# The last two sums of the seventh product's weights, at the front of VectorE's queue instead of its end

## The chip, the cores and the metric

The kernel runs on one core of one Trainium2 chip. The metric is the device time of one execution in microseconds (us). Lower is better.

## The reference

Every token is multiplied with the weights of all eight experts, and the results are added up with the softmax of the router's logits as factors:

```python
probs = softmax(router_logits)                    # 16 x 512 tokens, 8 experts
for e in range(8):
    output += probs[:, :, e:e+1] * np.matmul(x, expert_weights[e])   # 512 -> 2048 columns
```

Inputs and output are float32. Seen as one product, it is an 8192 x 4096 matrix (each token's 512 values times each of its eight factors) by a 4096 x 2048 matrix (the experts' weights below each other).

## The kernel before, in words

**Two levels of a seven-product scheme.** The big product is computed by a scheme of Strassen's kind: 2 x 2 blocks are multiplied with seven products instead of eight, and sums and differences of blocks are formed before and after. The outer level splits the tokens into blocks `a` and `b` of 256, the experts into two halves and the columns into two halves of 1024. Its products are called P1 to P7 here (`product(r, q)`, r = 1 to 7; q = 0 to 15 numbers the pairs of token blocks). The inner level does the same once more inside each product, with the seven steps `STEPS = (1, 5, 6, 2, 7, 3, 4)`. Each step is eight matmuls of 128 x 128 by 128 x 512 in float16 into one bank of PSUM. Some stages have a third level (`Thirds`); those near the change have none.

**Stages and slots.** `stages` is a list of pairs of products. `run(stage)` goes through the seven steps and takes one step of each product in turn, so a stage has 14 slots, the even ones of its first product and the odd ones of its second. Three stages matter here:

- stage k7: P6 for q = 15 (even slots) and P7 for q = 0 (odd slots), the first P7;
- stage k7+1: P4 for q = 0 (even) and P7 for q = 1 (odd);
- stage k7+2: P4 for q = 1 and P7 for q = 2.

In stage k7 slots 8 and 9 are step 7 of P6 and of P7, slots 12 and 13 are step 4.

**The right-hand side of a step** is a tile of 128 x 4096 float16, a block of weights or a difference of blocks (`inner_sums`). For P7 four blocks called t3 are fetched, and VectorE makes four differences of them: the sums for steps 5, 6, 7 and 4. Each is one instruction (`step`, L107). The sum for step 6 reads that for step 5, the sum for step 4 reads that for step 6, and the sum for step 7 is written over a block that the sum for step 5 reads. They are made once and serve all 16 P7.

**The left-hand side** (`Left`) is made anew for each product: two tiles `z` (experts' factors times x; for P7 a tile `u` of the other token block is subtracted from each), then `s2` (tile name `d`), the difference of the halves of the first, and `i` (a tile named `z` again, `z<-z,d` in the profile), the second minus `s2`. Step 6 reads `s2`, steps 7 and 3 read `i`.

**VectorE's queue.** VectorE runs its instructions in the order in which the kernel issues them. That order is written by a planner at build time. `later(cost, make, first=False)` puts a task at the end of `queue`, or with `first=True` at its front. `slack()`, once a slot, takes tasks off the front as long as VectorE's planned clock is behind TensorE's. `need(task)`, called by `Left.op` and `Right.op` right before a step's matmuls, takes everything off the front up to and including the task that the step reads. Additions that end a step (`post`, `h<-ps,h` in the profile) are issued directly, behind the step. `run` queues a stage's `i` tiles when the stage begins, and after the first slot (`queue_lefts`) the left sides of the next stage; both go to the end of the queue.

**Loads.** SyncE's queue issues the loads of x and factors (`xT`, `pT`) for the stage after next at slot 1 (`start_loads`), and the base blocks that a product's results are added to (`Base.fetch`, tile `h`). The last base block of P7 for q = 0, (1, 0), is issued at slot 3 of stage k7, behind those loads. `xT` and `pT` share a pool of 10 buffers, and a load waits until VectorE has read the buffer's old contents. ScalarE's queue issues the loads of P4's weights, 1 MB each (`turnover(k7, 0, 4, "t4")`, `fetch_w`, L164), at slots 1, 4, 7, 10 and 13 of stage k7 and at slot 2 of the next. In the built program the DMAs of these two queues take eight completion counters in turn, and a DMA waits until the one that had its counter before has landed. GpSimd's queue issues the stores of results (`out_dram<-h`).

Nearly all of VectorE's work has line 107 (`tt`), all steps' matmuls have line 130 (`mm`), and the tiles tell them apart. What the diff touches:

Of the kernel before, what the change touches and what calls it, by code (L numbers as in the profile page):

```python
# [31 lines left out]
def kernel(  # L32
# [73 lines left out]
    def tt(o, a, b, op):  # L106
        dve(nc.vector.tensor_tensor(out=o, in0=a, in1=b, op=op))  # L107
# [15 lines left out]
    def bank():  # L123
        return psum.tile([P, NB], f32, name="ps", tag="ps")

    def bank2():
        return psum.tile([P, NB], f32, name="pt", tag="pt", bufs=2)
# [6 lines left out]
    def new_w():  # L134
        return wpool.tile([P, K8, NB], f16, name="w", tag="w")

    def new_u():
        return zpool.tile([P, K8, HQ], f16, name="u", tag="u", bufs=1)

    def new_z():  # L140
        return zpool.tile([P, K8, HQ], f16, name="z", tag="z")
# [25 lines left out]
    def inner_sums(b, t7=None):  # L167

        w = {1: b[0, 0], 2: b[1, 0], 3: b[1, 1], 7: t7 or b[0, 1]}

        def step(p, x, y):
            if p not in w:
                w[p] = new_w()
            tt(w[p], x, y, SUB)
        return w, {5: lambda: step(5, b[0, 1], b[0, 0]), 6: lambda: step(6, b[1, 1], w[5]),
                   4: lambda: step(4, b[1, 0], w[6]), 7: lambda: step(7, b[1, 1], b[0, 1])}
# [145 lines left out]
    for n in range(2):  # L322
        ps = [bank2() if n == 0 and j < 2 else bank() for j in range(4)]
        for e in range(HE):
# [4 lines left out]
            if n == 0 and e == 2:  # L329
# [3 lines left out]
                w, sums = inner_sums(b11, new_w())  # L333
# [36 lines left out]
    def flush(task):  # L370
        while task is not None and not task.done:
            queue.popleft().run()

    def need(task):
        if task is not None and not task.done:
            flush(task)
            clock["pe"] = max(clock["pe"], clock["dve"])

    def later(cost, make, first=False):
        t = Task(cost, make)  # L380
        (queue.appendleft if first else queue.append)(t)
        return t
# [58 lines left out]
    def times(z, k, xb, pb):  # L441
        tt(z.rearrange("p (e c) t -> p e c t", e=2), xb.t.unsqueeze(1).to_broadcast([P, 2, C, HQ]),
           pb.t[:, ds(2 * k, 2)].unsqueeze(2).to_broadcast([P, 2, C, HQ]), MUL)

    class Left:
# [6 lines left out]
        def make(self, k):  # L452
            if self.of is not None:
                need(self.of.task[k])
            t = self.t[k] = new_z()
            times(t, k, self.xb, self.pb)
            if self.less is not None:
                u = new_u()
                times(u, k, *self.less)
                tt(t, t, u, SUB)  # L460
            if self.of is not None:
                tt(t, self.of.t[k], t, SUB)
            if self.kept is not None:
                tt(t, t, self.kept.t[:, ds(k * K8, K8), :], SUB)
# [80 lines left out]
    class Right:  # L545
# [6 lines left out]
            self.w, sums = inner_sums(b)  # L552
            return sums

        def queue_sum(self, sums, p):
            self.task[p] = later(2.29, sums[p])

        def op(self, p):
            need(self.task.get(p))
# [94 lines left out]
    def at(stage, slot, make):  # L654
        hooks.setdefault((stage, slot), []).append(make)

    def add(*products):
        stages.append(products)
        return len(stages) - 1


    right = {r: Right() for r in (2, 5, 6, 7, 4, 3)}
# [33 lines left out]
    def product(r, q, **how):  # L696
        left, loads = left_of(r, q)
        lefts[r, q] = left
        p = None
        if r == 1:  # L700
            def sink(tn, o):
                pool(kept_rows(q)(tn), o)
            p = Product(right[1], left, sink)
        elif r == 2:
            if q >= ON_BASE:
                bases[2, q] = Base(kept_rows(q))
            p = Product(right[2], left, to_out(q, 0, 0), bases.get((2, q)))
        elif r == 5:
            bases[6, q] = m1 = Base(kept_rows(q))
            m1.task = {}  # L710

            p = Product(right[5], left, to_out(q, 1, 0))
        elif r == 6:
            m1 = bases[6, q]

            def base(tn):
                need(m1.task[tn])
                return m1.t[tn]
            p = Product(right[6], left, to_out(q, 0, 1), base)
        elif r == 7:  # L720
            base = bases[7, q] = Base(lambda tn: out_rows(q, 0, 1, tn))
            p = Product(right[7], left, to_out(q, 1, 1), base)
        elif r == 4:
            p = Product(right[4], left, to_out(q, 1, 0, accum_op=ADD), products[7, q].o.__getitem__)
        else:
            p = Product(right[3], left, to_out(q, 0, 1, accum_op=ADD), **how)
        p.loads = loads
        products[r, q] = p
        return p
# [137 lines left out]
    k7 = add(some, product(7, 0))  # L867
# [79 lines left out]
    for kn, where in zip(((0, 0), (0, 1), (1, 1), (1, 0)), ((1, 8), (3, 2), (5, 0), (5, 9))):  # L947
        at(*where, lambda kn=kn: cast21(kn))

    def sums_at(stage, slot, r, of, ps):  # L950
        def go():
            if right[r].w is None:
                right[r].sums = right[r].build(of)
            for p in ps:
                right[r].queue_sum(right[r].sums, p)
        at(stage, slot, go)
    sums_at(ND - 1, 3, 2, b21, (5,))
    sums_at(ND - 1, 5, 2, b21, (6,))
    sums_at(ND - 1, 7, 2, b21, (7,))
    sums_at(ND - 1, 12, 2, b21, (4,))  # L960
    ODD = 0, 1
    for i, (kn, e) in enumerate((kn, e) for kn in (ODD, (0, 0), (1, 1), (1, 0)) for e in range(2)):
        stage = ND + i - 2 if kn != ODD else 2 + 2 * i
        wedge_at(stage, 2, kn, e, (stage + 1, 0))

    def fetch_at_w(stage, slot, of, what, kn):
        at(stage, slot, lambda: of.__setitem__(kn, fetch_w(what, kn)))
# [101 lines left out]
    def turnover(stage, place, r, raw, every=3):  # L1069

        right[r].w = {}

        def fetch(p):
            if p in RAW:
                right[r].w[p] = fetch_w(raw, RAW[p])
            else:
                right[r].w[p] = fetch_w((r, p), (0, 0))
        if every == 3:
            at(stage - 1, 9, lambda: fetch(1))
        for i, p in enumerate(STEPS[every == 3:]):  # L1080
            at(*slots_after(stage, place + 1, every * i), lambda p=p: fetch(p))
    t3 = {}
    for slot, kn in zip((0, 2, 4, 6), ORDER):
        fetch_at_w(k7 - 1, slot, t3, "t3", kn)
    for stage, slot, p in ((k7 - 1, 10, 5), (k7 - 1, 13, 6), (k7, 3, 7), (k7, 7, 4)):
        sums_at(stage, slot, 7, t3, (p,))
    turnover(k7, 0, 4, "t4")
    turnover(k3 - 1, 1, 3, "b22", 2)

# [119 lines left out]
```

## Time and profile before

| | us |
|---|---|
| time, median of 3 runs | 1374.52 (1374.25 to 1374.65) |
| the profiled execution's own time | 1374.57 |
| its span, first to last instruction | 1372.5 |
| TensorE busy (matmuls) | 1355.9 |
| VectorE busy | 1130.7 |
| ScalarE, GpSimd busy | 258.8, 435.8 |

Times in the profile are counted from the first instruction. `z<-xT,pT` means that an instruction writes a tile of that name and reads the two others; buffer numbers are left out. In a timeline the first two columns are start and duration, and an idle time of the engine ahead of the instruction stands in brackets with what ended it. One instruction's duration reaches some 0.08 us into the next one's, so that what an instruction costs in a row of them is the distance of two starts. A matmul's modelled end lies 0.16 us behind the start of the next.

### The profile page before, as it was taken

What the parts mean: (1) busy time and instruction counts of PE and PEld (TensorE: products, weight loads), DVE (VectorE), ACT (ScalarE), POOL (GpSimd) and SP (SyncE); (2) the same over time, 40 slices, a digit from 0 to 9 for tenths busy, and PEclk for the clock granted to TensorE, in tenths of its full rate; (3) what the DMA queues carried; (4) which work ended last, traced back from release to release, by engine and by line L of the source; (5) the groups of instructions that cost most, each with busy time, mean ns of one, the idle gap of its engine ahead of it and who ended that gap; (6) DMA issues with size and microseconds to landing.
All of it is one profiled execution on the core that took longest, in us unless ns stands there. A gap on an engine that the chain in (4) does not pass through costs nothing.

```text
span 1372.5 us, 18682 instructions
## 1 busy us (share of the span) xinstructions
PE 1355.9 (99%) x6822; PEld 665.0 (48%) x6822; DVE 1130.7 (82%) x1365; ACT 258.8 (19%) x517; POOL 435.8 (32%) x667
## 2 busy tenths in 40 slices
PE   9999999999999999999999889999999999999998
PEld 4555545565544444444444334444444444556554
DVE  7876677878899888887878987888989888898884
ACT  3233313242211111111111100000000000233331
POOL 3223323332222323223221113344443434233341
PEclk9999999999999999999999989999999999999999
DMA  9999979898999999999987977999999999999997
GB/s 183 245 218 266 246 222 227 256 243 248 255 333 290 281 311 288 281 262 298 299 265 266 345 257 192 229 255 264 255 265 234 270 259 308 336 304 247 207 159 136
DMA packets 190683, 353.55 MB, mean 258 GB/s; under 512 B 52992, under 2 KB 81920, under 8 KB 185856
## 3 DMA queue, kind: packets, MB, share of 16 engines
q0 software_dynamic: 89824, 189.31, 59.1%
q1 hardware_dynamic: 97456, 139.86, 33.8%
q10 hardware_dynamic: 3312, 23.20, 4.4%
q8 instruction: 53, 0.87, 0.3%
q14 instruction: 38, 0.31, 0.1%
HBM read 208.44 MB, written 180.55 MB: 283 GB/s over the span
## 4 chain that ended last, share of the span: by engine, by line
PE 98%; DVE 1%; DMA 0%; issue 0%; POOL 0%; ACT 0%; DVEq 0%; POOLq 0%
PE ps L130 74%; PE pt L130 24%; DVE z L107 1%; DMA w<-in_x_dram 0%; DVE h L107 0%; DVE u L107 0%; DVE w L107 0%; DVE d L107 0%; DVE z L255 0%; POOL w L121 0%; ACT h L1155 0%; DVE lg L295 0%; DVEq L107 0%; POOLq L1193 0%
## 5 line engine op out<-in xcount | busy, mean ns | idle before, releaser
L130 PE MATMUL ps<-w,z 128*128 128x512 f16 (+1 forms) x3768 | 822.1, 375 | 10.9 <-DVE w L107 10.9
L130 PEld LDWEIGHTS <-z 128*128 128x128 f16 x5272 | 516.0, 98 | 590.5 <-issue 13.7
L121 POOL DMA_DIRECT2D out_dram<-h x380 | 256.0, 706 | 698.8 <-ACT h L614 274.2
L130 PE MATMUL pt<-w,z 128*128 128x512 f16 (+1 forms) x1504 | 317.9, 359 | 0.0
L107 DVE TENSOR_TENSOR z<-xT,pT 128x2048 f16<-128x2048 f16 x220 | 265.9, 1216 | 3.5 <-PE pt L130 2.6
L107 DVE TENSOR_TENSOR h<-ps,h 128x512 f32<-128x512 f32 x248 | 168.9, 687 | 95.4 <-PE ps L130 75.3
L130 PE MATMUL ps<-w,d 128*128 128x512 f16 x880 | 199.1, 379 | 0.0
L601 ACT COPY h<-ps 128x512 f32<-128x512 f32 x118 | 69.2, 586 | 420.2 <-PE ps L130 394.3
L130 PEld LDWEIGHTS <-d 128*128 128x128 f16 x880 | 86.0, 98 | 100.1
L107 DVE TENSOR_TENSOR z<-z,d 128x2048 f16<-128x2048 f16 x110 | 131.8, 1216 | 0.0
L107 DVE TENSOR_TENSOR h<-pt,h 128x512 f32<-128x512 f32 x125 | 85.2, 687 | 50.9 <-PE pt L130 49.2
L107 DVE TENSOR_TENSOR w<-w 128x1024 f16<-128x1024 f16 (+2 forms) x105 | 112.3, 1086 | 1.9 <-PE ps L130 1.0
L614 ACT COPY h<-ps 128x512 f32<-128x512 f32 x50 | 29.3, 586 | 402.5 <-PE ps L130 364.6
L107 DVE TENSOR_TENSOR d<-z 128x1024 f16<-128x1024 f16 x110 | 74.6, 684 | 4.5 <-PE ps L130 3.4
L107 DVE TENSOR_TENSOR ps<-ps,h 128x512 f32<-128x512 f32 (+1 forms) x88 | 51.0, 582 | 26.7 <-PE ps L130 23.3
L597 ACT COPY h<-ps 128x512 f32<-128x512 f32 x95 | 52.6, 605 | 70.7 <-PE ps L130 70.7
L121 POOL DMA_DIRECT2D kept<-h x56 | 30.7, 548 | 93.9 <-ACT h L601 53.8
L121 POOL DMA_DIRECT2D out_dram<-kept x56 | 56.4, 1042 | 12.2 <-DMA out_dram<-h 6.3
L593 ACT COPY ps<-ps 128x512 f32<-128x512 f32 x59 | 33.6, 570 | 121.0 <-PE ps L130 65.3
L107 DVE TENSOR_TENSOR ps<-pt,h 128x256 f32<-128x256 f32 x36 | 15.5, 432 | 38.7 <-PE pt L130 26.6
L107 DVE TENSOR_TENSOR h<-h 128x512 f32<-128x512 f32 (+2 forms) x69 | 45.1, 675 | 1.1 <-DMA h<-kept 0.9
L107 DVE TENSOR_TENSOR z<-z,u 128x2048 f16<-128x2048 f16 x36 | 44.1, 1225 | 1.2
(73 smaller groups left out, 543.9 us busy)
## 6 DMA issues: line engine op xcount, KB each, us to landing
out_dram<-h POOLq DMA_DIRECT2D x380, 256.0 KB, 7.3
pT<-p_dram SPq DMA_DIRECT2D x126, 256.0 KB, 7.2
w<-wd ACTq DMA_DIRECT2D x22, 1024.0 KB, 9.5
xT<-x SPq DMA_DIRECT2D x80, 256.0 KB, 7.5
h<-kept SPq DMA_DIRECT2D x72, 256.0 KB, 8.2
h<-out_dram SPq DMA_DIRECT2D x68, 256.0 KB, 6.0
w<-in_expert_weights_dram POOLq DMA_DIRECT2D x33, 512.0 KB, 10.2
kept<-h POOLq DMA_DIRECT2D x56, 256.0 KB, 5.2
```

What stands on the lines that cost most here:

```text
L107: dve(nc.vector.tensor_tensor(out=o, in0=a, in1=b, op=op))
L121: note(nc.gpsimd.dma_start(out=o, in_=i, **how))
L130: note(nc.tensor.matmul(ps, z, w, start=start, stop=stop, skip_group_check=True))
L593: act(nc.scalar.copy(self.banks["b"], x))
L597: act(nc.scalar.copy(o[tn], q if p == 5 else x))
L601: act(nc.scalar.copy(o[TN[p]], b if p == 2 else x))
L614: act(nc.scalar.copy(o[tn], b))
```

## The change

The sums for P7's steps 7 and 4 are queued one slot later than before (4 and 8 instead of 3 and 7 of stage k7), and at the front of the queue instead of its end. As a task at the front could be run ahead of a sum that it depends on, `queue_sum` now runs that one first if it is still queued. The sums for steps 5 and 6, and those of the other products, are queued as before.

```diff
-        def queue_sum(self, sums, p):
-            self.task[p] = later(2.29, sums[p])
+        def queue_sum(self, sums, p, first=False):
+            def make():
+                flush(self.task.get({6: 5, 7: 5, 4: 6}.get(p)))
+                sums[p]()
+            self.task[p] = later(2.29, make, first)
...
-    def sums_at(stage, slot, r, of, ps):
+    def sums_at(stage, slot, r, of, ps, first=False):
...
-                right[r].queue_sum(right[r].sums, p)
+                right[r].queue_sum(right[r].sums, p, first)
...
-    for stage, slot, p in ((k7 - 1, 10, 5), (k7 - 1, 13, 6), (k7, 3, 7), (k7, 7, 4)):
-        sums_at(stage, slot, 7, t3, (p,))
+    for stage, slot, p in ((k7 - 1, 10, 5), (k7 - 1, 13, 6), (k7, 4, 7), (k7, 8, 4)):
+        sums_at(stage, slot, 7, t3, (p,), p in (7, 4))
```

Built, both programs have the same instructions in the same order on TensorE, ScalarE, GpSimd and SyncE. On VectorE the order differs from stage k7 on for about four stages and is then the same again. This is the order from the end of step 6 of P6 in stage k7, one instruction or group each:

| before | after |
|---|---|
| end of P6 step 6 | end of P6 step 6 |
| a subtraction `h<-h` for P6 | **sum 7** |
| `i` of P6 | end of P7 step 6 |
| end of P7 step 6 | `h<-h` for P6 |
| `i` of P7 | `i` of P6 |
| P4's left: `z`, `d`, `z` | **sum 4** |
| end of P6 step 7 | end of P6 step 7 |
| P7's next left: `z`, `u`, `z<-z,u`, `d` | `i` of P7 |
| and `z`, `u`, `z<-z,u` | P4's left: `z`, `d` |
| **sum 7**, **sum 4** | end of P7 step 7 |
| end of P7 step 7 | P4's left: `z` |
| ends of P6, P7 step 3, P6, P7 step 4 | end of P6 step 3 |
| `i` of P4 | P7's next left: `z`, `u`, `z<-z,u` |
| end of P4 step 1 | ends of P7 step 3, P6 step 4, P7 step 4 |
| `i` of the next P7 | end of P4 step 1 |
| end of the next P7's step 1 | next P7's left: `d`, `z`, `u`, `z<-z,u` |
| and so on | end of the next P7's step 1, and so on |

The completion counters come out otherwise too. Before, the load of the weights for P4's step 7 has the counter of the base block (1, 0) of P7 for q = 0 and waits for its landing. After, the loads for P4's steps 7, 3 and 4 have counters of loads that were issued at the beginning of stage k7. In both programs the loads for steps 3 and 4 also wait for their buffers, until P6's steps 7 and 3 have read what is in them.

## Prediction

> **What bounds the kernel now.** I read the busy times first, then the waits, then TensorE's timeline around the one long wait.
>
> ```profile
> PE 1355.9 (99%) x6822; PEld 665.0 (48%) x6822; DVE 1130.7 (82%) x1365; ACT 258.8 (19%) x517; POOL 435.8 (32%) x667
> PE 98%; DVE 1%; DMA 0%; issue 0%; POOL 0%; ACT 0%; DVEq 0%; POOLq 0%
> PE ps L130 <- DVE w L107: 10.9, 1, 10.9
> ```
>
> TensorE (PE) is busy for 1355.9 of 1372.5 us and makes up 98% of the chain that ended last. Of its 16.6 us of idle time one single wait is 10.9: matmuls that waited for a tile `w` written by VectorE, a sum of weights. Only time in which TensorE stands or runs slowly can be won.
>
> ```profile
> 772.29 3.62 PE L130 MATMUL pt<-w,z 128*128 128x512 f16 x16
> 775.74 3.62 PE L130 MATMUL ps<-w,d 128*128 128x512 f16 x16
> 779.20 5.34 PE L130 MATMUL ps<-w,z 128*128 128x512 f16 x24
> 795.46 3.57 PE L130 MATMUL ps<-w,z 128*128 128x512 f16 x8 [10.92 <-DVE w L107]
> 798.82 3.79 PE L130 MATMUL pt<-w,z 128*128 128x512 f16 x16
> 802.46 7.07 PE L130 MATMUL ps<-w,z 128*128 128x512 f16 x32
> ```
>
> From 772.29 to 779.20 four slots take 6.91 us, 1.73 each. The two rows with `pt` and `d` are slots 2 to 5 of stage k7; so slots 6, 7 and 8 start at 779.20, 780.93 and 782.65, and slot 9, step 7 of P7, is due at 784.38. It starts at 795.46, **11.08 us late**. Then slots 9 to 11 take 7.00 us (795.46 to 802.46) where three take 5.18, another **1.82 us**. The clock says why:
>
> ```profile
> 784.00:788.00 4.00, 0.54 (x3) 0.14 (x2) 3.97 (x5) 0.00 (x0) 0.81 (x2) 1.00 0.94 341
> 788.00:792.00 4.00, 0.00 (x0) 0.00 (x0) 3.93 (x5) 0.00 (x0) 0.00 (x0) 0.62 1.03 373
> 796.00:800.00 4.00, 4.00 (x13) 1.45 (x11) 2.30 (x2) 0.00 (x0) 0.00 (x0) 0.60 1.01 424
> ```
>
> The third number from the right is the granted clock. A mean of 0.62 in 788 to 792 is full speed until 789.0 and half behind it; 0.60 in 796 to 800 is half until 799.2. So the clock fell 4.4 us after TensorE's last matmul had ended (779.20 + 5.34 = 784.54) and came back 10.2 us later. The whole stall costs 12.90 us.
>
> What VectorE (DVE) did meanwhile:
>
> ```profile
> 770.67 2.29 DVE L107 TENSOR_TENSOR w<-w 128x4096 f16<-128x4096 f16 x1
> ...
> 777.67 0.69 DVE L107 TENSOR_TENSOR h<-ps,h 128x512 f32<-128x512 f32 x1
> 778.28 0.68 DVE L107 TENSOR_TENSOR h<-h 128x512 f32<-128x512 f32 x1
> 778.88 1.22 DVE L107 TENSOR_TENSOR z<-z,d 128x2048 f16<-128x2048 f16 x1
> 780.01 0.68 DVE L107 TENSOR_TENSOR h<-ps,h 128x512 f32<-128x512 f32 x1
> 780.61 1.22 DVE L107 TENSOR_TENSOR z<-z,d 128x2048 f16<-128x2048 f16 x1
> 781.75 1.22 DVE L107 TENSOR_TENSOR z<-xT,pT 128x2048 f16<-128x2048 f16 x1
> 783.00 0.69 DVE L107 TENSOR_TENSOR d<-z 128x1024 f16<-128x1024 f16 x1
> 783.61 1.22 DVE L107 TENSOR_TENSOR z<-xT,pT 128x2048 f16<-128x2048 f16 x1
> ...
> 789.60 1.22 DVE L107 TENSOR_TENSOR z<-xT,pT 128x2048 f16<-128x2048 f16 x1
> 790.73 1.22 DVE L107 TENSOR_TENSOR u<-xT,pT 128x2048 f16<-128x2048 f16 x1
> 791.98 1.22 DVE L107 TENSOR_TENSOR z<-z,u 128x2048 f16<-128x2048 f16 x1
> 793.12 4.49 DVE L107 TENSOR_TENSOR w<-w 128x4096 f16<-128x4096 f16 x2
> 799.07 0.69 DVE L107 TENSOR_TENSOR h<-ps,h 128x512 f32<-128x512 f32 x1 [1.46 <-PE ps L130]
> ...
> 806.11 0.69 DVE L107 TENSOR_TENSOR h<-ps,h 128x512 f32<-128x512 f32 x1 [1.03 <-PE ps L130]
> ```
>
> It worked without a break. Sum 7 (first of the two `w<-w` at 793.12, done at 795.41) stood behind everything that the queue held, the next stage's left sides above all, which nobody needed yet.
>
> **The change, part by part.** It moves two instructions; none is added or removed, and the new `flush` finds the sums for steps 5 and 6 done (the first ran at 770.67). What an instruction costs in a row is the distance of starts: `h` 0.60 (778.28 to 778.88), `z` 1.13 to 1.14 (778.88 to 780.01), `z` before a `d` or `z<-z,u` that reads it 1.25 (781.75 to 783.00), `d` 0.61, `w<-w` 2.20 (4.49 for two less 2.29).
>
> *Term A, stage k7.* The start at 777.67 (end of P6's step 6) is the last that both orders share. After it, by the order as built: sum 7 at 778.28, end of P7's step 6 at 780.48 (its matmuls are done at 779.20), `h<-h` 781.08, `i` of P6 781.68 to 782.90, sum 4 at 782.81, end of P6's step 7 at 785.01, `i` of P7 785.61 to 786.83. Sum 7 is early now, ready at 780.57. But the two sums cost 4.4 us of VectorE ahead of the two `i`, which steps 7 also read. Slot 8 was due at 782.65 and waits for `i` of P6 until about 782.95; slot 9 waits for `i` of P7 until about 786.88, so it starts **2.50 us late** instead of 11.08, after two short idles of 0.3 and 2.2. With all clocks full the time would be 1374.57 - 12.90 + 2.50 = 1364.2.
>
> *Term B, stage k7+1.* What is late next is the base block (1, 0), which the end of P7's step 4 adds to.
>
> ```profile
> 782.85 0.59 ACT L614 COPY h<-ps 128x512 f32<-128x512 f32 x1 [1.14 <-DMA xT<-x]
> 785.26 3.32 SPq L118 DMA_DIRECT2D h<-out_dram  x4
> DMA to landing us min/median/max: 6.1/6.4/6.9
> 781.13 0.33 ACTq L164 DMA_DIRECT2D w<-wd  x1
> DMA to landing us min/median/max: 9.1/9.1/9.1
> 792.23 9.03 ACTq L164 DMA_DIRECT2D w<-wd  x3
> DMA to landing us min/median/max: 7.6/8.7/9.9
> h<-kept SPq DMA_DIRECT2D x3, 256.0 KB, 13.5
> ```
>
> The rows are from the timelines of ScalarE and SyncE, each issue with the shortest, median and longest time to landing of its DMAs behind it; the last is from the DMA issues of 755 to 771. The block is the first of the four at 785.26 on SyncE's queue. It stands behind a `pT` load that waits until VectorE has made P4's second `z` (783.61 + 1.22 = 784.83). It took 6.9 and landed at 792.2, long before its use at 806.11. After the change P4's `z`, `d` and `z` stand behind the sums and the end of P7's step 7: 786.75, 788.00, then that end at 788.9 (slot 9's matmuls end at 788.61; VectorE follows about 0.25 later, as at 799.07), `z` 789.5 to 790.7. The block is issued 0.43 behind that as before, at about 791.1, 5.9 us later. Its use comes 10 us earlier: P7's step 4 ends at 795.5.
>
> The price of its lateness is read off VectorE's order: the block's addition stands ahead of the end of P4's step 1, the next P7's `d`, `z`, `u`, `z<-z,u` and the end of its step 1 (0.60 + 0.61 + 0.61 + 1.13 + 1.25 + 1.14, then 0.70). The end of P4's step 1 frees a bank for slot 4, and the last one the bank for the next P7's step 6, slot 5, due at 795.54 + 5 x 1.73 = 804.2. So the block must land by about **798.1**, 7.0 us after its issue. Later than that, TensorE loses each us in full.
>
> What will it take? From below, the 6.9 of the same load: B is 0. From above, the longest loads of such a block, 13.5 in the median of three in 755 to 771, when two weight loads also moved: B is 6.5. Before, only the weights for P4's step 2 (781.13, landed at 790.3) moved beside it; it landed 1.9 us behind them. The weights for steps 7 and 3 waited for the block itself (the row at 792.23). After, they don't: they are issued at about 783.4, behind the copy at 782.85, and at 785.0, when slot 8 ends; those for step 4 at 790.4, when slot 10 ends. Of the two at 792.23 and 792.9 the first took 7.6, the second 9.9: about 3 us more for each 1 MB that queues behind another. Two more ahead of the block put its landing at 790.3 + 6 + 1.9 = 798.2, B = 0.1; three at 801.3, B = 3.2; two stores of results that now come earlier add some 1.4 between them by size. I take about the middle of 0.1 and 4.6: **B = 2.4**, landing at 800.5.
>
> The weights themselves are in time: step 7 of P4 starts at 809.4, 26 us after its load's issue. ScalarE's loads now wait for less, and its next copies are for stage k7+1. GpSimd's stores follow VectorE's ends, which come earlier. From the fourth stage on the orders are the same, and all of TensorE's idle time but this wait is 5.7 us in the whole span, so later stages keep what is won.
>
> Sum: 1374.57 - 12.90 + 2.50 + 2.4 = **1366.6**. The median of the three runs is 1374.52, the same within 0.01%.
>
> A rule that bears on A: the Trainium skill, "TensorE: Matmul & The Clock Gate", Part 1, says that TensorE goes to half clock after an idle window of some 3.4 us. The trace agrees so far, with a fall 4.4 us into an idle of 10.9; no row shows an idle of 2 to 4 us. By this rule the new idles cost no clock, as the sum has it.
>
> **The rivals.**
> 1. *The base block is in time* (22%). For it: 6.9 us before, though weights moved beside it. Then B is 0 and the time 1364.2. Against it: two or three more MB are ahead of it. This is how it would go by the Trainium skill, "DMA: Bandwidth & Descriptors", Queues, rings and completion order: each DMA engine takes turns between the queues, packet by packet, so that weights on ScalarE's queue don't go first. The 13.5 us above speak against equal turns.
> 2. *The base block is as slow as the slowest* (10%), 11 to 13.5 us: B is 4 to 6.5, split over slots 4 and 5, 1368.2 to 1370.7.
> 3. *The clock falls already in the new idles* (6%), since 2.2 us is untested: half speed for 10.2 us costs up to 5.1: 1369.3 with B = 0, 1371.7 with 2.4.
> 4. *Slower* (3%): the block is so late that TensorE's idle in slot 4 passes the 4.4 us at which the clock fell. That idle is about the landing less 801.1, so it decides from a landing at 805.5 on, 14.4 us after the issue; then 7.4 of B and a half clock whose loss is partly hidden in slot 5's wait bring 1374; with 17 us it is 1377. No load here took so long.
> 5. *No effect* (3%), 1374.5: something other than the sums held slot 9. Against it: the wait names `w`, and the order as built has sum 7 fifteen instructions earlier.
>
> **How the numbers follow.** Forecast 56%, with its own range of 1364.5 to 1369 (B from 0.3 to 4.8). The range to hold 8 in 10 reaches down to the first rival and up into the second and third: 1363.8 to 1370. A change within 0.2% (2.7 us) cannot be told from none. Faster: forecast, first, nearly all of the second and third, 92%. Same: the rest of those, the fifth and a part of the fourth, 6%. Slower 2%.
>
> **What would show it.** Right: the 10.9 us wait of matmuls for `w` is gone; instead TensorE waits for a `z` at about 784.7, some 2.2 us, and about 20 us later again, with VectorE's `h<-ps,h` ahead of it held by a DMA `h<-out_dram`; the clock never falls between 780 and 810. Wrong: a granted clock under 1 there; a second idle of none or of over 5 us; a new wait beyond 815.

## The result, and the profile after

| | us | ratio to before, 95% interval |
|---|---|---|
| before, median of 20 executions | 1374.91 (1374.25 to 1377.48) | |
| after, median of 20 | **1369.59** (1366.53 to 1374.91) | 0.9961 [0.9953, 0.9969] |
| after once more, in a later measurement, median of 5 | 1368.09 (1367.22 to 1368.58), before there 1375.23 | 0.9947 [0.9934, 0.9959] |
| the profiled execution after | 1367.99, span 1366.0 | |

The kernel is faster by 0.4 to 0.5%. The waits of TensorE and VectorE between 700 and 900 us (total, times, longest) are these now:

```profile
DVE h L107 <- DMA h<-out_dram: 3.5, 1, 3.5
...
PE ps L130 <- DVE z L107: 2.0, 1, 2.0
...
PE ps L130 <- DVE ps L107: 1.3, 1, 1.3
```

The wait for `w` of 10.9 is gone. In its place stand a short one for a `z`, a short one for a bank of PSUM (`ps`), and one of VectorE for a base block. TensorE's timeline puts them in their places:

```profile
772.84 3.62 PE L130 MATMUL pt<-w,z 128*128 128x512 f16 x16
776.29 3.62 PE L130 MATMUL ps<-w,d 128*128 128x512 f16 x16
779.75 5.66 PE L130 MATMUL ps<-w,z 128*128 128x512 f16 x24
787.44 3.56 PE L130 MATMUL ps<-w,z 128*128 128x512 f16 x8 [2.04 <-DVE z L107]
790.79 3.69 PE L130 MATMUL pt<-w,z 128*128 128x512 f16 x16
794.32 7.07 PE L130 MATMUL ps<-w,z 128*128 128x512 f16 x32
801.22 3.62 PE L130 MATMUL pt<-w,z 128*128 128x512 f16 x16
804.68 1.89 PE L130 MATMUL ps<-w,d 128*128 128x512 f16 x8
807.83 1.89 PE L130 MATMUL ps<-w,d 128*128 128x512 f16 x8 [1.26 <-DVE ps L107]
```

These starts account for the whole difference, with 1.73 us a slot as before:

- Slot 2 of stage k7 starts at 772.84 instead of 772.29: 0.55 later, lost ahead of the stages that the change touches.
- Slots 6 to 8 start at 779.75 and last 5.66 instead of 5.34, an idle of 0.3 at slot 8. Slot 9 was due at 779.75 + 5.18 = 784.93 and starts at 787.44: **2.51 late**.
- Slots 9 to 11 take 6.88 (787.44 to 794.32) instead of 5.18: **1.70** of half clock.
- From 794.32 on, six slots take the 10.36 that they should. Slot 5 of stage k7+1 was due at 804.68 + 1.73 = 806.41 and starts at 807.83: **1.42 late** (1.26 of idle, and the 0.16 by which a modelled end lies behind the next start).

Together 2.51 + 1.70 + 1.42 = 5.63 stand where 12.90 stood. 12.90 - 5.63 - 0.55 = 6.7, and the profiled executions differ by 1374.57 - 1367.99 = 6.6.

VectorE's timeline shows what TensorE waited for:

```profile
778.22 0.69 DVE L107 TENSOR_TENSOR h<-ps,h 128x512 f32<-128x512 f32 x1 [0.58 <-PE ps L130]
778.83 2.28 DVE L107 TENSOR_TENSOR w<-w 128x4096 f16<-128x4096 f16 x1
...
782.23 1.22 DVE L107 TENSOR_TENSOR z<-z,d 128x2048 f16<-128x2048 f16 x1
783.36 2.29 DVE L107 TENSOR_TENSOR w<-w 128x4096 f16<-128x4096 f16 x1
785.57 0.68 DVE L107 TENSOR_TENSOR h<-ps,h 128x512 f32<-128x512 f32 x1
786.17 1.22 DVE L107 TENSOR_TENSOR z<-z,d 128x2048 f16<-128x2048 f16 x1
...
791.04 0.69 DVE L107 TENSOR_TENSOR h<-ps,h 128x512 f32<-128x512 f32 x1 [1.80 <-PE ps L130]
791.65 1.22 DVE L107 TENSOR_TENSOR z<-xT,pT 128x2048 f16<-128x2048 f16 x1
...
801.75 0.69 DVE L107 TENSOR_TENSOR h<-ps,h 128x512 f32<-128x512 f32 x1 [3.54 <-DMA h<-out_dram]
802.36 0.69 DVE L107 TENSOR_TENSOR ps<-ps,h 128x512 f32<-128x512 f32 x1
...
807.08 0.69 DVE L107 TENSOR_TENSOR ps<-ps,h 128x512 f32<-128x512 f32 x1
```

Sum 7 (778.83) stands ahead of both `i` (782.23 and 786.17) and sum 4 (783.36) ahead of the second, and slot 9 starts when that one is made. Some 15 us later the end of P7's step 4 (801.75) waits 3.54 for the base block (1, 0). The end of the next P7's step 1, at 807.08, frees the bank that slot 5 needs at 807.83. The block's issue on SyncE's queue, with its time to landing:

```profile
792.89 0.32 SPq L118 DMA_DIRECT2D pT<-p_dram  x1
793.30 2.52 SPq L118 DMA_DIRECT2D h<-out_dram  x4
DMA to landing us min/median/max: 8.3/8.3/8.3
```

It was issued at 793.30, right behind the `pT` load that waits for P4's second `z` (791.65 to 792.87), and landed at 801.6. On ScalarE's queue the weights for P4's steps 7, 3 and 4 had gone out before it, the first at 783.41 and the last by 783.41 + 9.74 = 793.15:

```profile
783.41 9.74 ACTq L164 DMA_DIRECT2D w<-wd  x3
```

The clock. The third number from the right is the granted clock, and the first pair is the length and TensorE's busy time:

```profile
780.69:784.10 3.41, 3.27 (x16) 1.30 (x15) 3.41 (x5) 1.17 (x2) 0.54 (x1) 1.00 1.02 416
784.10:787.51 3.41, 1.37 (x8) 0.47 (x6) 3.41 (x4) 0.00 (x0) 1.08 (x2) 1.00 0.99 400
787.51:790.92 3.41, 3.41 (x9) 1.23 (x10) 1.70 (x2) 0.00 (x0) 0.00 (x0) 0.50 1.03 420
790.92:794.34 3.42, 3.42 (x18) 1.51 (x17) 3.30 (x4) 0.00 (x0) 1.08 (x2) 1.00 0.99 414
```

One stretch of 3.41 us ran at half clock, and the stretch of 3.41 us before it held the whole idle of slot 9. That these stretches are no arbitrary cut is shown below.

### The profile page after: what moved, and what is told of

The parts are those of the page before. It is cut to its first block, busy times and chain, and to the rows that moved or that the text cites. A ratio compares the mean times of both kernels' runs of the same rounds, so it can differ in the third digit from the quotient of the medians.

```text
span 1366.0 us, 18685 instructions
## 1 busy us (share of the span) xinstructions
PE 1355.8 (99%) x6822; PEld 664.8 (49%) x6822; DVE 1130.1 (83%) x1365; ACT 258.7 (19%) x517; POOL 435.9 (32%) x667
## 4 chain that ended last, share of the span: by engine, by line
PE 97%; DVE 1%; DMA 1%; issue 0%; POOL 0%; ACT 0%; SPq 0%; DVEq 0%; POOLq 0%
PE ps L130 74%; PE pt L130 23%; DMA h<-out_dram 1%; DMA w<-in_x_dram 0%; DVE z L107 0%; DVE w L107 0%; DVE h L107 0%; DVE ps L107 0%; DVE u L107 0%; DVE z L255 0%; POOL w L121 0%; DVE d L107 0%; ACT h L1158 0%; SPq L118 0%; DVEq L107 0%
```

## The experiments

My theory of the result: the gain is the old stall less three terms, (A) the two sums stand ahead of the `i` tiles, (B) the base block lands late since weights for P4 move beside it, and (C) the idle of A lets the clock fall. The rivals were that the block lands late because of its own late issue or a slow load whatever moves beside it (against B), and that the top of the spread comes from somewhere else than stages k7 and k7+1. Each experiment starts from the changed kernel. All ratios are to the kernel before on the same chip.

**base_early: the base block a few slots earlier** (slot 0 of stage k7 instead of 3, ahead of the `pT` load that waits).

```diff
-        for slot, tn in zip((7, 9, 11, 17), INNER):
+        for slot, tn in zip((7, 9, 11, 14 if q == 0 else 17), INNER):
```

> The changed kernel, with the base block (1, 0) of P7 for q = 0 fetched three slots earlier, ahead of the loads that hold SyncE's queue up. Theory 1 (the second idle, at slot 5 of stage k7+1, is that block's late landing, and most of the spread of the times comes from it): VectorE's wait for the DMA h<-out_dram (3.5 us in the profile after) and TensorE's wait for a ps (1.3 us) are gone; the idles of 0.35 and 2.0 us at slots 8 and 9 stay. Time 1364.2 with a full clock, 1365.9 with 3.4 us of half clock; spread within about 2 us. Theory 2 (the spread comes from the clock, which falls after the idle at slot 9 in some executions and for different lengths): the spread stays, 1364 to 1369, and the median is above 1366. Theory 3 (something else): 1369.6 as in the changed kernel.

Measured: 1365.74 (1364.49 to 1366.76, 5 executions), ratio 0.9932 [0.9919, 0.9944]. Its profile (1364.49) has the two idles of term A unchanged, 0.3 and 2.04, and none at slot 5; the clock never fell there. With A alone the prediction had 1364.2. So B is real and is the base block.

**i_first: the two `i` tiles ahead of the sums.**

```diff
+    def i_first():
+        planned = clock["dve"]
+        for p in stages[k7]:
+            flush(p.left.task["i"])
+        clock["dve"] = planned
+    at(k7, 4, i_first)
     for stage, slot, p in ((k7 - 1, 10, 5), (k7 - 1, 13, 6), (k7, 4, 7), (k7, 8, 4)):
```

> The changed kernel, with the i tiles of P6 and P7 made at slot 4, ahead of both sums (the planner's clock is left as if they had not been, so that the order behind them stays close). The base block is fetched as in the changed kernel. Both theories: no idle at slots 8 and 9 of stage k7, and no fall of the clock there. Theory 1 (the block's landing makes the spread): it is used sooner still, VectorE waits for it and TensorE loses 1 to 5 us in stage k7+1; time 1363 to 1368, with a spread as in the changed kernel. Theory 2 (the clock makes it): the second idle stays near 1.4 to 2.5, time 1363 to 1364.5, and the spread is gone.

Measured: 1370.33 (1368.47 to 1371.74, 6), ratio 0.9965 [0.9953, 0.9978]. That is no gain over the change, and above what was expected. TensorE's timeline:

```profile
785.96 1.89 PE L130 MATMUL ps<-w,z 128*128 128x512 f16 x8 [0.35 <-DVE h L107]
...
802.77 1.89 PE L130 MATMUL ps<-w,d 128*128 128x512 f16 x8 [1.06 <-DVE ps L107]
807.50 3.30 PE L130 MATMUL ps<-w,d 128*128 128x512 f16 x8 [2.84 <-DVE ps L107]
```

The idle of 2.04 at slot 9 is gone, as meant. But the base block is not issued earlier by the same amount (792.61, landed 8.7 later at 801.3), while TensorE needs it 3.1 us earlier (slot 5 is due at 798.10 + 3 x 1.73 = 803.29 instead of 806.41), and so the idles behind it grow from 1.26 to 1.06 + 2.84. The second is long enough that the clock fell for 3.41 us behind it. In four of the six executions the mean clock was 0.996 or 0.997 (0.003 of 1366 us is 4.1 us lost; half clock behind the last matmul counts in that mean too), so probably more than one such stretch. What is won at one wait is given back at the next one.

**both: i_first and base_early together.**

> Both of the above: i tiles ahead of the sums, and the base block fetched three slots earlier. If the two idles and what follows from them (the clock) are all that was left of the stall of 12.9 us, nothing of it stays: no wait of TensorE over 0.4 us between 780 and 815 us, full clock throughout, 1374.7 - 12.9 = 1361.8, within 0.5, with a spread like that of the kernel before. If a further wait stands behind these, 1363 and more, and the profile names it.

Measured: 1363.86 (1362.78 to 1364.54, 4), ratio 0.9918 [0.9905, 0.9932]. So, by the medians, i_first is worth about 2 us once B is away (base_early to both; the two intervals overlap), and nothing while B is there. It missed the 1361.8 expected by 2, and VectorE's timeline has the cause:

```profile
803.64 0.70 DVE L107 TENSOR_TENSOR ps<-ps,h 128x512 f32<-128x512 f32 x1 [3.04 <-DMA h<-out_dram]
```

It is the end of the next P7's step 1, which now waits for the first base block of that product. The block was issued at 790.40 and took 13.1 us:

```profile
DMA to landing us min/median/max: 13.1/13.1/13.1
```

TensorE stood 1.81 us at slot 5 for it. The two blocks issued behind it took 14.1 and 14.5. The same three weight loads moved beside them, issued earlier here (783.63 to 788.80); the last of these took 13.1 us as well and landed at 801.9, 1.6 ahead of the block.

**weights_late: the weights for P4's steps 7, 3 and 4 issued behind the base blocks** (at slot 12 of stage k7, on GpSimd's queue). Nothing else is changed in the kernel's text, and the base block keeps its place.

```diff
-    def fetch_w(what, kn):
+    def fetch_w(what, kn, by=nc.scalar):
...
+        def by(p):
+            return nc.gpsimd if r == 4 and p in (7, 3, 4) else nc.scalar
...
-            at(*slots_after(stage, place + 1, every * i), lambda p=p: fetch(p))
+            n = 12 if r == 4 and p in (7, 3, 4) else place + 1 + every * i
+            at(*slots_after(stage, n, 0), lambda p=p: fetch(p))
```

> The changed kernel, with the loads of the weights for P4's steps 7, 3 and 4 moved from ScalarE's queue to GpSimd's and to slot 12 of stage k7, behind the results of P7's step 3, so that they move after the base block and not before or beside it. The block is issued as late as in the changed kernel (about 791 us). Theory A (the block is late because 2 to 3 MB of weights move ahead of it): it lands within 7 us, VectorE's wait for it is under 1 us, TensorE's idle at slot 5 is gone; 1364.2 to 1366 with the clock. Theory B (only the late issue matters, and weights on another queue don't hold it up): VectorE waits for the block about as long as in the changed kernel (3.5 us), TensorE idles 1 us or more, 1366 to 1370. If the weights come too late by this, P4's step 7 (slot 8 of the next stage) waits for a DMA w<-wd instead.

Measured: 1364.91 (1363.90 to 1366.27, 5), ratio 0.9927 [0.9915, 0.9940]. The base block was issued at 792.29, as late as in the profiles of the changed kernel (791.05 to 793.30), and its time to landing and VectorE's wait for it are:

```profile
DMA to landing us min/median/max: 5.7/5.7/5.7
```

```profile
798.14 0.69 DVE L107 TENSOR_TENSOR h<-ps,h 128x512 f32<-128x512 f32 x1 [0.50 <-DMA h<-out_dram]
```

The idle at slot 5 is gone. With the same late issue, the three weight loads were worth 2.6 us of landing (8.3 to 5.7) against the first profile of the changed kernel and more against the others. While the block was under way the 16 DMA engines were busy for 0.99 of the time at 332 GB/s in the changed kernel (793.30 to 801.60), and for 0.75 at 192 GB/s here (792.29 to 798.00). This tells the theory from its rival: the lateness comes from what moves beside the block, not from the issue alone. Term A is as before, and the clock fell once in the profile (1365.74). Two of the five executions have a mean clock of 0.999 and took 1365.74 and 1366.27; three have 1.000 and took 1363.90 to 1364.91. The means differ by 1.7, the price of one stretch at half clock. In base_early the clock doesn't sort the times so: four executions with 1.000 lie between 1364.49 and 1366.76, and what they differ by isn't shown.

**all_three: i_first, base_early and weights_late together.**

> The i tiles ahead of the sums, the base block fetched three slots earlier, and P4's weights for steps 7, 3 and 4 loaded late on GpSimd's queue. In the run with the first two alone one wait of TensorE was left (1.8 us at slot 5 of stage k7+1, behind a base block of the next P7 that took 13.2 us to land). If weights ahead of the base blocks are the cause of that too, no wait over 0.4 us is left between 780 and 815 us: the whole 12.9 us are won, 1375.0 - 12.9 = 1362.1 in the median, with a spread under 1.5 us. If it is something else, the wait stays and the time is that of the two alone, 1363.9.

Measured: **1362.46** (1361.73 to 1364.19, 4), ratio 0.9908 [0.9895, 0.9922]. This beats the kernel before and the changed kernel, whose interval beside it on the same chip was [0.9934, 0.9959]; from `both` it can't be told. In the profiled execution, the slowest of the four, TensorE waits for another sum of P7's weights, that for step 5:

```profile
775.89 1.89 PE L130 MATMUL pt<-w,z 128*128 128x512 f16 x8 [1.04 <-DVE w L107]
786.76 1.89 PE L130 MATMUL ps<-w,z 128*128 128x512 f16 x8 [0.35 <-DVE h L107]
```

VectorE was held 3.06 us at 771.74 by blocks `h<-kept` ahead of that sum. In stage k7+1 no wait over 0.3 us is left.

**sum7_alone: only the first of the two sums at the front**, the sum for step 4 at the end of the queue at slot 7 as before.

```diff
-    for stage, slot, p in ((k7 - 1, 10, 5), (k7 - 1, 13, 6), (k7, 4, 7), (k7, 8, 4)):
-        sums_at(stage, slot, 7, t3, (p,), p in (7, 4))
+    for stage, slot, p in ((k7 - 1, 10, 5), (k7 - 1, 13, 6), (k7, 4, 7), (k7, 7, 4)):
+        sums_at(stage, slot, 7, t3, (p,), p == 7)
```

> Only the sum for step 7 goes to the front; the sum for step 4 is queued as in the kernel before (slot 7, at the end). Slot 9 is then late by 0.3 us at most, since the second sum no longer stands ahead of the i tile of P7. But the sum for step 4 stands behind the next stage's left sides, done at about 801; step 4 of P7, slot 13, is due at about 791.6: TensorE waits some 9.6 us there for a w, the clock falls, and the time is 1374 to 1375. If the sum for step 4 is not needed at the front, 1364 or less.

Measured: 1374.61 (1374.00 to 1375.22, 10), ratio 0.9995 [0.9986, 1.0004]. All of the gain is gone, and the wait is only moved to the sum for step 4, at slot 13:

```profile
801.51 7.80 PE L130 MATMUL ps<-w,z 128*128 128x512 f16 x24 [9.52 <-DVE w L107]
```

**front_3_7: both sums at the front, but at the slots 3 and 7 of the kernel before.**

```diff
-    for stage, slot, p in ((k7 - 1, 10, 5), (k7 - 1, 13, 6), (k7, 4, 7), (k7, 8, 4)):
+    for stage, slot, p in ((k7 - 1, 10, 5), (k7 - 1, 13, 6), (k7, 3, 7), (k7, 7, 4)):
```

> Both sums at the front as in the changed kernel, but queued at slots 3 and 7 as in the kernel before. By VectorE's order as built both sums then stand ahead of the i tile of P6, so that the whole of term A, some 2.5 us, falls on slot 8 in one idle; the base block's addition stands as in the changed kernel. Time as in the changed kernel within 2 us, 1366 to 1371: the front of the queue is what matters, the slot only says where the 2.5 us are lost. If the later slots matter, 1372 or more.

Measured: 1366.47 (1365.19 to 1367.01, 4), ratio 0.9937 [0.9922, 0.9952], which its interval doesn't separate from the changed kernel's beside it. So it is the front of the queue that makes the gain; what the slots add to the time is not told apart. Its profile (1365.19) has one idle of 2.34 at slot 8, none at slot 5 and no half clock. The base block was late here too (8.6 to land), but VectorE's order behind it is another one:

```profile
800.13 0.69 DVE L107 TENSOR_TENSOR h<-ps,h 128x512 f32<-128x512 f32 x1 [3.88 <-DMA h<-out_dram]
...
802.21 0.70 DVE L107 TENSOR_TENSOR ps<-ps,h 128x512 f32<-128x512 f32 x1 [0.19 <-DMA h<-out_dram]
802.82 1.22 DVE L107 TENSOR_TENSOR z<-xT,pT 128x2048 f16<-128x2048 f16 x1
```

The end of the next P7's step 1 (802.21), which frees the bank for slot 5, stands ahead of that product's `z`, `u`, `z<-z,u` and not behind them as in the changed kernel. So the same wait of VectorE cost TensorE nothing. Against the expectation, the slots do change the order behind the block, and term B depends on that order as well as on the landing.

**after_again and after_look1 to 3: the changed kernel itself**, timed again and profiled four more times, to see which of the terms vary.

> The changed kernel once more, for its spread beside the others on one chip, and for a second profile. Term A (0.35 and 2.0 us at slots 8 and 9) is fixed by VectorE's order and must be the same to 0.1. The landing of the base block should differ from the 8.3 us of the first profile by some us, and TensorE's idle at slots 4 and 5 of stage k7+1 with it, one to one. If the times again reach from 1366.5 to 1372 or more and the clock explains under 2 us of it, the block's landing is the larger part.

> The changed kernel, one profiled execution, to see the same execution's time and landing together. In the two profiles so far the base block took 8.3 and 10.0 us to land and TensorE lost 1.3 and 2.6 us behind it. If the landing makes the spread, time = 1364.2 + TensorE's idle at slots 4 and 5 of stage k7+1 + 0 or 1.7 for the clock, within 0.7 us, whatever the time is.

> As after_look1, another execution: time = 1364.2 + TensorE's idle at slots 4 and 5 of stage k7+1 + 0 or 1.7 for the clock, within 0.7 us. If a time over 1371 comes with idles that add up to less, something outside these two stages varies.

> As after_look1, a third execution: time = 1364.2 + TensorE's idle at slots 4 and 5 of stage k7+1 + 0 or 1.7 for the clock, within 0.7 us.

| profile of the changed kernel | its time | idle at slot 9 | idle at slot 5 | base block, issue to landing | half clock |
|---|---|---|---|---|---|
| after | 1367.99 | 2.04 | 1.26 | 8.3 | 3.4, behind slot 9's idle |
| after_again | 1368.31 | 2.03 | 2.57 | 10.0 | 3.4, behind slot 9's |
| after_look1 | 1368.21 | 2.03 | 2.11 | 9.1 | 3.4, behind slot 5's |
| after_look2 | 1369.06 | 2.04 | 2.21 | 9.8 | 3.4, behind slot 9's |
| after_look3 | 1368.32 | 2.03 | 1.40 | 9.6 | 3.4, behind slot 9's |

A is the same in all five to 0.01 us. B varies from 1.3 to 2.6, with the load's landing and with the half clock, which delays the block's use too (after_look3 lost less than after_look1, though its block took longer). In all five the block landed 0.1 to 1.1 us behind the third weight load, which was issued between 0.5 us ahead of the block and 0.6 us behind it. With full clock, A alone gives 1364.2 (the working of the prediction); adding the idle at slot 5 and the 1.7 of the half clock gives 1367.2, 1368.5, 1368.0, 1368.1 and 1367.3. The times measured lie from 0.2 below to 1.0 above these. The 0.7 that was expected held for after_look1 (0.2) and not for after_look2 and after_look3 (1.0 each), so that up to 1 us lies outside the sum. None of the five profiles caught an execution above 1370. Of the 20 of the first measurement ten were, most with the same mean clock (0.999) as others below 1369, so that the clock doesn't tell them apart. What they lost, and where, stays open, and so does a part of the median of 1369.59, which is 1.1 above the highest of the five sums.

**When the clock falls.** An idle of 2.03 or 2.04 was followed by half clock in some profiles and not in others, so its length alone doesn't decide. The moments of the falls do. In the changed kernel's profile the clock also falls behind the last matmul, and the two falls, with the return between them, are in these rows:

```profile
787.40:787.60 0.20, 0.16 (x1) 0.11 (x2) 0.20 (x1) 0.00 (x0) 0.00 (x0) 0.78 0.94 389
790.80:791.00 0.20, 0.20 (x2) 0.15 (x1) 0.00 (x0) 0.00 (x0) 0.00 (x0) 0.69 0.54 225
1364.20:1364.40 0.20, 0.00 (x0) 0.00 (x0) 0.00 (x0) 0.00 (x0) 0.00 (x0) 0.92 0.00 0
```

A mean of 0.78 over 0.20 us is full clock for 0.112 and half for the rest, a fall at 787.512; 0.69 puts the return at 790.924, 3.412 later, and 0.92 the other fall at 1364.368. The falls lie 576.856 apart, which is 169 times 3.4133, the length of that stretch within what the rows resolve. In after_look3 slot 9 starts 0.22 later, but both falls come 1.38 later (788.896 and 1365.748), again 576.85 apart; in weights_late they are 576.85 apart too. So the clock is decided at the edges of windows of 3.41 us that run on through the whole span, wherever the matmuls stand. The fall behind the last matmul then gives the edges in the profiles without a fall in between, by counting windows back. In base_early (fall at 1363.272) an edge is at 786.42, in the middle of slot 9's idle, 785.12 to 787.16:

```profile
783.01:786.42 3.41, 1.98 (x9) 0.70 (x8) 3.41 (x4) 0.58 (x1) 0.69 (x2) 1.00 1.00 408
786.42:789.83 3.41, 2.67 (x13) 1.26 (x14) 3.24 (x5) 0.00 (x0) 0.39 (x1) 1.00 1.04 426
789.83:793.24 3.41, 3.41 (x18) 1.52 (x17) 3.41 (x4) 0.00 (x0) 1.08 (x2) 1.00 1.01 402
```

TensorE was busy for 1.98 and 2.67 us of the two windows, and the clock stayed. In the changed kernel's profile the whole idle lay in one window with 1.37 of work, and the next one ran at half clock. The profile after_look2 has both cases:

```profile
784.77:788.19 3.42, 1.38 (x7) 0.48 (x6) 3.42 (x4) 0.00 (x0) 0.74 (x2) 1.00 0.96 367
788.19:791.60 3.41, 3.41 (x10) 1.22 (x8) 2.10 (x4) 0.00 (x0) 0.00 (x0) 0.50 1.01 423
805.25:808.67 3.42, 1.47 (x7) 0.58 (x6) 3.39 (x4) 0.00 (x0) 0.00 (x0) 1.00 0.52 149
808.67:812.08 3.41, 3.15 (x15) 1.46 (x15) 3.41 (x6) 0.00 (x0) 0.00 (x0) 1.00 0.47 136
```

The profiles of the change and its variants together, each with the windows that had the least work at an idle:

| TensorE busy in a window of 3.41 | kernels | clock in the next window |
|---|---|---|
| 0.58 | i_first (slot 5) | 0.50 |
| 1.30 | after_look1 (slot 5) | 0.50 |
| 1.37 to 1.39 | after, after_again, after_look2, after_look3, weights_late (slot 9) | 0.50 |
| 1.47 | after_look2 (slot 5) | 1.00 |
| 1.57, 1.61 | after_again (slot 5), both (slot 5) | 1.00 |
| 1.77 to 1.98 | front_3_7, after_look1 (slot 9), base_early | 1.00 |

At full clock the bound lies between 1.39 and 1.47 us of work, or 2.02 and 1.94 of idle, in one window. An idle of 2.04 costs 1.7 us if it lies in one window, and nothing if an edge cuts more than a tenth of a us off it; where the edges lie differs from one execution to the next. The chance by it is about (3.41 - 2.04 + 0.1) / 3.41 = 0.4; of the seven profiles with this idle at slot 9, five had the half clock. These are readings of ten profiles; no kernel was made to shift the idle alone.

## Why the prediction was right, and where it was off

The forecast was 1366.6 and a gain; the time is 1369.59 (1368.09 in the later measurement), inside the range, 1.5 to 3.0 above the forecast.

- **The stall of 12.90 goes.** Right. sum7_alone shows that it takes both sums: with one of them the wait of 9.52 and the half clock stand at the other.
- **Term A, 2.50.** Right as a mechanism and in its size: slot 9 starts 2.51 late, behind idles of 0.3 and 2.04, in every profile of the change.
- **Term B, 2.4, from the base block behind the weights.** Right as a mechanism: base_early and weights_late each take it away from a different side. Idle at slot 5 was 1.3 to 2.6 in five profiles. Two errors met in it: the block was issued 2.2 later than I had it (793.30 instead of 791.1, of which 0.55 is the later stage and the rest the half clock at slot 9, which delays the end of P7's step 7; after_look1, with full clock there, has 791.05), but the same half clock also delayed its use. The sum counted the loads issued ahead of the block; after_look3 shows that the order of issue doesn't decide it.
- **"By this rule the new idles cost no clock, as the sum has it."** This is the step that failed. The term was set to nothing and measured 1.7, in all five profiles of the change. It is the third rival in a third of its size: I gave it 6% and priced it at up to 5.1, by the 10.2 us of half speed of the trace of before. There the idle covered more than two windows and the half clock lasted three; an idle of 2.04 spoils one window and costs one. "The clock never falls between 780 and 810" was wrong. By the row of 784.10 to 787.51 no idle window is needed: 1.37 us of work in one didn't keep the clock.
- **Rival 1, the block in time** by turns between the queues, didn't come: it took 8.3 to 10.0 with the weights beside it and 5.7 without. The Trainium skill, "DMA: Bandwidth & Descriptors", Queues, rings and completion order, has the queues take turns; the runs show that the turns don't keep a load of 256 KB free of loads of 1 MB on another queue. Going first by issue is not it: in after_look3 the third weight load, four times the size, was issued 0.6 us behind the block and landed 0.1 ahead of it. How the loads share the engines isn't shown.
- **Rivals 2, 4 and 5** didn't come. The 13.1 us of rival 2 was seen, but in `both`, for the next product's block.
- **What the sum didn't have:** 0.55 us of later arrival at stage k7 in the profile, and a spread of 8 us between executions where before has 3. The terms explain 3 to 5 of it: B varies by 1.3, the clock costs from nothing to 1.7, or 3.4 if both idles fell badly. The rest is open.

## What to carry to other kernels

When a task is moved to the front of a queue, list what it now stands ahead of, and then follow the next load that is issued behind that work: here two sums of 4.4 us in front delayed the release of a buffer, and so the issue of the loads behind it (the base block 8 us, 785.26 to 793.30), and 2 MB and more of weights, which had waited for that block's completion counter before, moved beside it. Fixes of waits that stand one behind the other don't add up: i_first gained nothing alone and, by the medians, 2 us once the next wait was gone. Price an idle time of a matmul stream by its place too, and not by its length alone.

## What the runs showed of the hardware

- The clock went by windows of 3.41 us that run through the whole span: 1.39 us of work or less in one meant half clock in the next, 1.47 or more didn't. The Trainium skill, "TensorE: Matmul & The Clock Gate", Part 1, has free-running windows of 3413 ns; the trace agrees (169 of them between two falls). It puts the fall behind an idle window; here 2.02 us of idle in a window was enough.
- The way back asks for more: in sum7_alone a window at half clock with 1.60 us of work was followed by another at half clock (the window and the next one):

```profile
799.71:803.12 3.41, 1.60 (x4) 0.56 (x4) 1.75 (x1) 0.00 (x0) 0.00 (x0) 0.50 1.06 386
803.12:806.54 3.42, 3.42 (x9) 1.21 (x8) 1.42 (x2) 0.00 (x0) 0.43 (x1) 0.50 0.54 225
```

- A load of 256 KB landed 5.7 us after its issue with the DMA engines busy for 0.75 of the time (weights_late), 8.3 to 10.0 with three weight loads of 1 MB issued ahead of it or up to 0.6 us behind it on another queue, and 13.1 to 14.5 for three other blocks in `both`.
